# Twelve feed-forward tiles of the first two token blocks computed jointly by seven quarter products, and the softmax mixer's two heads interleaved

## The chip, the cores and the metric

The kernel runs on one core of a Trainium2 chip. The metric is the device time of one execution in microseconds (us); lower is better. Engines are named as in the profile: PE (TensorE matmul), PEld (its weight load), DVE (VectorE), ACT (ScalarE), POOL (GpSimd) and SP (SyncE, which issues DMAs).

## The reference

One layer of a hybrid decoder, for 2048 tokens of 1024 features in float32, with 16 meta tokens ahead of them:

```python
def hybrid_layer(h, pos, norm_mix_w, w_in, w_gate_up, b_gate, gla_norm_w, sinks,
                 w_out, norm_ff_w, w_ff1, w_ff2):
    u = rmsnorm(h, norm_mix_w)
    proj = u @ w_in
    gq, gk, gv, gr, glr, sq, sk, sv = jnp.split(proj, split_points, axis=-1)
    o_gla = gla_mixer(gq, gk, gv, gr, glr, w_gate_up, b_gate, gla_norm_w)   # gated linear attention, chunks of 64
    o_swa = swa_mixer(sq, sk, sv, sinks, pos)       # softmax in a window of 128, 8 heads in 2 groups
    h = h + jnp.concatenate([o_gla, o_swa], axis=-1) @ w_out
    f = rmsnorm(h, norm_ff_w)
    return h + jnp.square(jax.nn.relu(f @ w_ff1)) @ w_ff2                    # 1024 -> 4096 -> 1024
```

The result is the final rmsnorm of that, without the meta tokens.

## The kernel before

**Precision.** Every operand of a large product is split into a high and a low part, and a product of one 128-row k tile is three matmuls of 512 columns: high x high, high x low, low x high (`mm3`, lines 158 to 160). The split of a weight is one ACT pass (`wh`, line 123) and one DVE pass (`wl`, line 124).

**Blocks.** The tokens are four blocks of 512. The feed-forward layer has 32 tiles of 128 hidden units. For a block, a tile is `up` (8 k tiles, 24 matmuls into `psd`; then DVE `fr`, ACT square and high part, DVE low part `hid`, lines 1376 to 1384), and `down` takes groups of 8 tiles: for each of 8 output tiles 24 matmuls and a DVE add into `h` (line 1405).

**Stages, in the order of time.** Blocks 0 and 1 are projected with seven products of quarters (to 186 us). Then two mixer streams start, `gla` and `swa`, Python generators whose every `yield` is a place where the driver puts the next large product between; they run until 1147 us. Beside them go the projection of blocks 2 and 3 (`u`), the trunk of block 0 (output projection, up, down; 485 to 1006 us) and the first part of block 1's trunk (1006 to 1373 us). Then comes the tail: the output projection of blocks 2 and 3 (1373 to 1461), the last group of block 1's `down` as a cover for the preparation (to 1506), and blocks 2 and 3 jointly by quarters: `up` (1506 to 1811), `down` (class `Second`, 1811 to 2078) and a last piece.

**Quarters.** A product of a 2 x 2 arrangement (two blocks of tokens or two halves) by 2 x 2 quarters of the weight is done as seven products of sums of quarters in place of eight (up into `psq`, down into `psw`). DVE and ACT make the sums: for `up` those of the weight (`r`) and of the activations (`ops`), for `down` the operands `b` (hidden units' sums, which are stored to DRAM as `hops` by `to_ops` and loaded again by `load_b`) and the weight's (`rw`, line 2108). `close_0` to `close_2` finish a pair of tiles, `evict` (line 2165) adds a product into two or more results. The order within these stages is written out by hand: `W2.job(step, ...)` puts a load or a sum into a step, and `chain` gives the order of the first sums with a time for each.

**Softmax mixer.** For each of 16 blocks of 128 tokens and for each of two kv heads: `swa_scores` (four pairs of score matmuls `sc`, exponentials, on POOL four scalings `p`, line 997), then `swa_values` (transposes `tr` and `trm`, split into `ph` and `pl`, POOL's `affine_select` for the triangle, line 1026, three kinds of value matmuls into `pv`). The GLA mixer's POOL work is the copies `qpad` (line 1215) and eight scalings `AT` (line 1231). The score, transposed and norm tiles (`sc`, `tr`, `psn`) share two PSUM buffers.

**Queues.** Each engine runs its instructions in the order in which they were written; all DMAs are issued by SP in order.

Of the kernel before, what the change touches and what calls it, by code (L numbers as in the profile page):

```python
# [17 lines left out]
P = 128  # L18
# [12 lines left out]

F_SK, F_SQ, F_Q, F_K, F_R = 0, 1, 5, 7, 9
NFEAT = 13


class Layer:
# [80 lines left out]
    def split_w(self, src, n=1024):  # L117
        nc, wp = self.nc, self.wp
        raw = wp.tile([P, 1024], F32, name="raw", tag="raw")[:, :n]
        nc.sync.dma_start(out=raw, in_=src)  # L120
        wh = wp.tile([P, 1024], F32R, name="wh", tag="wh")[:, :n]
        wl = wp.tile([P, 1024], F32R, name="wl", tag="wl")[:, :n]
        nc.scalar.activation(wh, raw, AF.Copy)  # L123
        nc.vector.tensor_tensor(wl, raw, wh.bitcast(F32), ALU.subtract)  # L124
        return wh, wl
# [49 lines left out]
    def meta_prep(self, cp):  # L175
# [8 lines left out]
        for kt in range(KT):  # L184
            t = cp.tile([P, 48], F32R, name=f"um{kt}", tag=f"um{kt}")
# [6 lines left out]
        for kt in range(KT // 2):  # L192
            t = cp.tile([P, 48], F32R, name=f"umd{kt}", tag=f"umd{kt}")
# [731 lines left out]
    def swa(self, sp):  # L925
# [10 lines left out]
        yield  # L936
        yield
        yield
        for b in range(nblk):
# [60 lines left out]
    def swa_values(self, kv, sp, p, pm, lhs, oT):  # L1000
        nc = self.nc
        pt = self.px.tile([P, NB], F32, name="trm", tag="sx")

# [3 lines left out]
        for g in range(4):  # L1007
            d, s = self.ptm[:, g * P : (g + 1) * P], self.pm4.bitcast(F32)
            nc.scalar.activation(d, s, AF.Copy, scale=self.hmask[:, g : g + 1])
        pt = self.px.tile([P, NB], F32, name="tr", tag="sx")  # L1010
        c0 = 0 if len(lhs) == 2 else P + NM
        for g in range(4):
            nc.tensor.transpose(pt[:, g * P : (g + 1) * P], p[:, g, c0 : c0 + P], self.ident)
        ph = sp.tile([P, NB], F32R, name="ph", tag="ph")
        pl = sp.tile([P, NB], F32R, name="pl", tag="pl")
        nc.scalar.activation(ph, pt, AF.Copy)
        nc.vector.tensor_tensor(pl, pt, ph.bitcast(F32), ALU.subtract)
        yield
        yield
        pv = self.pm.tile([P, NB], F32, name="pv", tag="pv", bufs=1)  # L1020
        for i, v in enumerate(lhs):
            if i:

                for t in (ph, pl):
                    tv = t.rearrange("p (a b) -> p a b", a=4)
                    nc.gpsimd.affine_select(
                        tv, tv, pattern=[[0, 4], [1, P]], compare_op=ALU.is_ge, fill=0.0, base=0, channel_multiplier=-1
                    )
                yield
                yield  # L1030
                yield
            for t in (ph, pl):
                nc.tensor.matmul(pv, lhsT=v[:, kv, :], rhs=t, start=i == 0 and t is ph, stop=False)  # L1033
        nc.tensor.matmul(pv, lhsT=self.vm[:, kv, :], rhs=self.ptm, start=False, stop=True)
        ol = sp.tile([64, NB], F32, name="ol", tag="pl")
        nc.scalar.activation(ol, pv[64:P, :], AF.Copy)
        nc.vector.tensor_tensor(
            oT[64 * kv : 64 * kv + 64].rearrange("p a b -> p (a b)"), pv[0:64, :], ol, ALU.add
        )
        yield  # L1040
# [166 lines left out]
    def gla_pair(self, c, gp, qk, v):  # L1207
# [24 lines left out]
        yield  # L1232
        yield
# [97 lines left out]
    def out_proj(self, blk, mx, halloc, acc, after=None):  # L1331
# [3 lines left out]
        for m in range(KT):  # L1335
            w = self.split_w(a["wo"][m].rearrange("p k c -> p (k c)"))
# [3 lines left out]
            if self.finish and m == 0:  # L1340
                next(self.finish)
# [11 lines left out]
    def trunk(self, blk, ahead_of, hid_pair, last):  # L1353
# [6 lines left out]
        accs = [self.acc_tile()]  # L1360
        units = []
        hs = yield from self.out_proj(blk, mx[0], self.halves("h", F32, units), accs[0])
# [5 lines left out]
        hid = [[None] * 8 for _ in range(4)]  # L1368

        def up(ff):  # L1370
            w = self.split_w(a["w1"][ff].rearrange("p k c -> p (k c)"))
            ps = yield from self.product(w, lambda k: f[k])
            if not rb:
                rb.append(self.rstd_bc(accs[0]))
# [3 lines left out]
            if self.finish:  # L1378
                next(self.finish)
                if ff == 3:  # L1380
                    self.finish = None
            h, l = hid_pair(ff)
            nc.scalar.activation(h, r, AF.Copy)
            nc.vector.tensor_tensor(l, r, h.bitcast(F32), ALU.subtract)  # L1384
            hid[ff // 8][ff % 8] = (h, l)
            yield

        def final(acc):

            rf = self.rstd_bc(acc)  # L1390
            yield
            for m in range(KT):
                h = hs[m]
                nc.vector.scalar_tensor_tensor(h, h, self.nfin[:, m : m + 1], rf, ALU.mult, ALU.mult)
                nc.sync.dma_start(out=self.out[blk, :, m, :], in_=h)
                if m % 2:
                    yield

        def down(g):
            if g == 3:  # L1400
                accs[0] = self.acc_tile()
            for m in range(KT):
                w = self.split_w(a["w2"][g, m].rearrange("p k c -> p (k c)"))
                ps = yield from self.product(w, lambda k: hid[g][k])
                nc.vector.tensor_tensor(hs[m], hs[m], ps, ALU.add)
                if g == 3:
                    self.sumsq_add(hs[m], accs[0], m, fast=True)
                if g == (2 if last else 3) and m >= 4:
                    self.ahead = self.ahead or ahead_of()
                    for _ in range(3):  # L1410
                        next(self.ahead[0], None)
                yield

        yield from up(0)
        for g in range(4):
            for t in range(1, 8):
                yield from up(8 * g + t)
            if g < 3:
                yield from up(8 * g + 8)
            if last and g == 3:  # L1420
                continue
            self.half_way = last and g == 2
            yield from down(g)

        if last:
            self.left = hs, units, hid[3]
        else:
            self.finish = final(accs[0])


    def tail_pair(self, blks, ax, hb, pq):
# [3 lines left out]
        hs1, units1, hid3 = self.left  # L1435
        ahead, mx = self.ahead
        for _ in ahead:
            pass
        self.ahead = None
        lo_half, up_half = slice(0, NB), slice(NB, 1024)  # L1440
        two = lambda t: t.rearrange("p (k c) -> p k c", k=2)
        accs = [self.acc_tile() for _ in blks]
        hu, rb = [[], []], []
        ops = {n: [] for n in range(1, 8)}
        spots = {1: [ax] * 4, 2: [ax] * 4, 6: [ax] * 4, 5: [hb] * 4, 7: [ax] * 4, 4: [hb] + [None] * 3, 3: [None] * 4}

        def op_hi(n, src):
            h, l = self.unit("oh", F32R, spots[n].pop(0)), self.unit("ol", F32R, spots[n].pop(0))
            nc.scalar.activation(h, src, AF.Copy)
            for c in (lo_half, up_half):  # L1450
                ops[n].append((h[:, c], l[:, c]))
            return lambda: nc.vector.tensor_tensor(l, src, h.bitcast(F32), ALU.subtract)

        def normed(t, j):
            nc.vector.tensor_tensor(two(t), two(t), rb[j].unsqueeze(1).to_broadcast([P, 2, NB]), ALU.mult)
# [4 lines left out]
        def after(j):  # L1460
            done = []

            def then(m, h):
# [4 lines left out]
                if m == KT - 1:  # L1468
                    scale(m, h)
                if j == 1:  # L1470
# [11 lines left out]
                    elif m == 4:  # L1482
                        op_hi(2, hu[0][2])()
                        op_hi(2, hu[0][3])()

            return then

        for j in range(2):
            yield from self.out_proj(blks[j], mx[j], self.halves("h", F32, hu[j]), accs[j], after(j))


        cov_raw, cov_w = {}, {}

        def cov_load(t):
            cov_raw[t] = self.wp.tile([P, 1024], F32, name="raw", tag="raw")
            nc.sync.dma_start(out=cov_raw[t], in_=a["w2"][3, t].rearrange("p k c -> p (k c)"))

        def w_hi(src):
            wh = self.wp.tile([P, 1024], F32R, name="wh", tag="wh")
            wl = self.wp.tile([P, 1024], F32R, name="wl", tag="wl")  # L1500
            nc.scalar.activation(wh, src, AF.Copy)  # L1501
            return (wh, wl), lambda: nc.vector.tensor_tensor(wl, src, wh.bitcast(F32), ALU.subtract)

        def cov_split(t):
            cov_w[t], lo = w_hi(cov_raw[t])
            lo()

        cov_load(0)
        cov_load(1)
        cov_split(0)  # L1510
        with self.tc.manual_schedule():
            self.tail_ordered(
                blks, ax, hb, pq, hu, rb, accs, ops, op_hi, normed, w_hi, cov_load, cov_split, cov_w, two,
            )

    def tail_ordered(
        self, blks, ax, hb, pq, hu, rb, accs, ops, op_hi, normed, w_hi, cov_load, cov_split, cov_w, two
    ):
        nc, a = self.nc, self.a
        hs1, units1, hid3 = self.left  # L1520
# [9 lines left out]
        def w_load(j, i):  # L1530
            t = W.setdefault(j, {})[f"r{i}"] = raw_tile("r")
            nc.sync.dma_start(out=t, in_=a["w1"][2 * j + i].rearrange("p k c -> p (k c)"))
# [43 lines left out]
        def sum_1(u):  # L1576
            t1[u] = self.unit("t1", F32, ax)
# [9 lines left out]
        def sum_4(u):  # L1587
# [4 lines left out]
        chain = [  # L1592
            (3.0, 0, lambda: rb.append(self.rsqrt_of(psn))),
            (1.23, 0, lambda: normed(b12[0], 1)),
            (1.23, 0, lambda: normed(b12[1], 1)),
            (1.23, 0, lambda: normed(b22[0], 1)),
            (1.23, 0, lambda: normed(b22[1], 1)),
# [673 lines left out]
```

## Time and profile before

| | |
|---|---|
| median of 3 runs | 2134.22 us (2134.05 to 2135.95) |
| the profiled execution | 2136.22 us, of which the span of its instructions is 2134.5 us |
| mean granted TensorE clock | 0.996 |
| PE busy | 2116.9 us, 10283 instructions |
| DVE, ACT, POOL busy | 1497.7, 1035.7, 160.0 us |
| HBM read and written | 227.64 and 69.86 MB, 139 GB/s |

A busy engine is one with an instruction under way. Matmuls overlap one another, so that the mean duration of one is not the time it adds; the distance between starts is. The granted clock is the share of full speed that TensorE was given in a stretch.

### The profile page before, as it was taken

What the parts mean: (1) busy time and instruction counts of PE and PEld (TensorE: products, weight loads), DVE (VectorE), ACT (ScalarE), POOL (GpSimd) and SP (SyncE); (2) the same over time, 40 slices, a digit from 0 to 9 for tenths busy, and PEclk for the clock granted to TensorE, in tenths of its full rate; (3) what the DMA queues carried; (4) which work ended last, traced back from release to release, by engine and by line L of the source; (5) the groups of instructions that cost most, each with busy time, mean ns of one, the idle gap of its engine ahead of it and who ended that gap; (6) DMA issues with size and microseconds to landing.
All of it is one profiled execution on the core that took longest, in us unless ns stands there. A gap on an engine that the chain in (4) does not pass through costs nothing.

```text
span 2134.5 us, 28244 instructions
## 1 busy us (share of the span) xinstructions
PE 2116.9 (99%) x10283; PEld 1785.6 (84%) x10283; DVE 1497.7 (70%) x2535; ACT 1035.7 (49%) x1969; POOL 160.0 (7%) x284
## 2 busy tenths in 40 slices
PE   9999999999999999999999999999999999999998
PEld 7987799888888888888888888888888888888887
DVE  7867856777977778788864445466867776785876
ACT  6524545446664646466652323453544545333434
POOL 0000212111111212121110000000000000000000
PEclk9999999999999999999999999999999999999999
DMA  6436333435333333334423334644345557754422
GB/s 241 142 117 230 114 98 114 131 127 166 96 115 103 112 95 112 98 118 153 138 84 104 99 97 152 201 135 136 125 162 182 173 176 262 293 175 141 146 70 79
DMA packets 148795, 299.42 MB, mean 140 GB/s; under 512 B 14384, under 2 KB 62256, under 8 KB 148656
## 3 DMA queue, kind: packets, MB, share of 16 engines
q1 hardware_dynamic: 148656, 297.62, 42.9%
q8 instruction: 81, 1.33, 0.2%
q14 instruction: 58, 0.48, 0.1%
HBM read 227.64 MB, written 69.86 MB: 139 GB/s over the span
## 4 chain that ended last, share of the span: by engine, by line
PE 94%; DVE 3%; DMA 1%; ACT 1%; issue 0%; SPq 0%; POOL 0%; DVEq 0%; ACTq 0%
PE psd L158 17%; PE psd L160 17%; PE psd L159 17%; PE psq L160 6%; PE psq L158 6%; PE psq L159 6%; PE psw L158 4%; PE psw L159 4%; PE psw L160 4%; PE psv L625 2%; PE lv L1191 2%; PE pv L1033 1%; PE psd L431 1%; PE psd L432 1%; PE psd L433 1%; PE sc L972 1%
## 5 line engine op out<-in xcount | busy, mean ns | idle before, releaser
L123 ACT ACTIVATE wh<-raw 128x1024 fp32r<-128x1024 f32 (+1 forms) x175 | 184.3, 1053 | 348.0 <-PE psd L160 320.2
L124 DVE TENSOR_TENSOR wl<-raw,wh 128x1024 fp32r<-128x1024 f32 (+1 forms) x175 | 215.9, 1234 | 47.5 <-ACT wh L123 47.2
L158 PE MATMUL psd<-f,wh 128*128 128x512 f32 x512 | 203.3, 397 | 0.0
L158 PE MATMUL psd<-hid,wh 128*128 128x512 f32 x512 | 202.4, 395 | 0.0
L160 PE MATMUL psd<-hid,wh 128*128 128x512 f32 x512 | 199.9, 390 | 0.4 <-DVE hid L1384 0.4
L160 PE MATMUL psd<-f,wh 128*128 128x512 f32 x512 | 199.9, 390 | 0.0
L159 PE MATMUL psd<-f,wl 128*128 128x512 f32 x512 | 199.7, 390 | 0.0
L159 PE MATMUL psd<-hid,wl 128*128 128x512 f32 x512 | 199.5, 390 | 0.0
L158 PE MATMUL psw<-bh,wh 128*128 128x512 f32 x392 | 152.5, 389 | 0.0
L159 PE MATMUL psw<-bh,wl 128*128 128x512 f32 x392 | 152.5, 389 | 0.0
L160 PE MATMUL psw<-bl,wh 128*128 128x512 f32 x392 | 152.5, 389 | 0.0
L158 PE MATMUL psq<-oh,wh 128*128 128x512 f32 x384 | 149.8, 390 | 0.0
L160 PE MATMUL psq<-ol,wh 128*128 128x512 f32 x384 | 149.4, 389 | 0.0
L159 PE MATMUL psq<-oh,wl 128*128 128x512 f32 x384 | 149.4, 389 | 0.0
L158 PE MATMUL psd<-u,wh 128*128 128x512 f32 x320 | 131.0, 411 | 0.7 <-ACT wh L310 0.7
L159 PE MATMUL psd<-u,wl 128*128 128x512 f32 x320 | 127.3, 398 | 0.0
L160 PE MATMUL psd<-u,wh 128*128 128x512 f32 x320 | 127.1, 397 | 0.0
L1501 ACT ACTIVATE wh<-rw 128x1024 fp32r<-128x1024 f32 x49 | 52.0, 1061 | 149.7 <-PE psw L160 132.9
L160 PEld LDWEIGHTS psd<-hid,wh 128*128 128x128 f32 x512 | 96.1, 188 | 21.6 <-DVE hid L1384 0.8
L160 PEld LDWEIGHTS psd<-f,wh 128*128 128x128 f32 x512 | 96.1, 188 | 20.9
L158 PEld LDWEIGHTS psd<-f,wh 128*128 128x128 f32 x512 | 96.2, 188 | 19.3 <-issue 0.5
L159 PEld LDWEIGHTS psd<-f,wl 128*128 128x128 f32 x512 | 96.2, 188 | 19.2 <-issue 0.5
(422 smaller groups left out, 5071.1 us busy)
## 6 DMA issues: line engine op xcount, KB each, us to landing
raw<-w SPq DMA_DIRECT2D x132, 512.0 KB
b<-hops SPq DMA_DIRECT2D x49, 512.0 KB
raw<-wo SPq DMA_DIRECT2D x32, 512.0 KB
r<-w SPq DMA_DIRECT2D x32, 512.0 KB
rw<-w2q SPq DMA_DIRECT2D x28, 512.0 KB
hops<-t SPq DMA_DIRECT2D x42, 256.0 KB
feat<-st SPq DMA_DIRECT2D x36, 256.0 KB
raw<-wf SPq DMA_DIRECT2D x17, 512.0 KB
```

Of the source, the lines that this page charges most:

```text
L123: nc.scalar.activation(wh, raw, AF.Copy)
L124: nc.vector.tensor_tensor(wl, raw, wh.bitcast(F32), ALU.subtract)
L158: nc.tensor.matmul(ps, lhsT=wh, rhs=ah, start=first, stop=False, skip_group_check=skip)
L159: nc.tensor.matmul(ps, lhsT=wl, rhs=ah, start=False, stop=False, skip_group_check=skip)
L160: nc.tensor.matmul(ps, lhsT=wh, rhs=al, start=False, stop=last, skip_group_check=skip)
L431: nc.tensor.matmul(ps, lhsT=ah, rhs=wh, start=kt == 0, stop=False)
L432: nc.tensor.matmul(ps, lhsT=ah, rhs=wl, start=False, stop=False)
L433: nc.tensor.matmul(ps, lhsT=al, rhs=wh, start=False, stop=kt == KT - 1)
L625: nc.tensor.matmul(ps, lhsT=x, rhs=y[:, w], start=new and i == 0 and k == 0 and n == 0, stop=i == 1 and k == 1 and n == 2, skip_group_chec ...
L972: nc.tensor.matmul(ps, lhsT=qh, rhs=self.kr[:, 2 * kv, win], start=True, stop=False)
L1191: nc.tensor.matmul(ps[:, at : at + P], lhsT=k[:, hp, j * P : (j + 1) * P], rhs=ql[:, :, :, 1, :], start=True, stop=True)
L1501: nc.scalar.activation(wh, src, AF.Copy)
```

## The change

Blocks 0 and 1 now do only 20 of the 32 tiles on their own (`PLAIN`). Block 0's groups are 8, 8 and 4 tiles; block 1's are 8, 4 and 8. The hidden units of block 1's first group are stored to DRAM (`held`) and used at the tail as the cover that its last group was before; its last group is now the cover of a new joint stage. That stage does tiles 20 to 31 of both blocks by quarters with the routine of the tail (`ordered`, `Second` with one group of three pairs). Its inputs, the residuals after the output projection, are stored by the trunk (`hmid`, and `hpart` after its own down products), and are loaded, scaled, normed and split in `prefetch`, which takes a step in each of block 1's ups 15 to 19. The sums of hidden units go through `hops_j`. In its last steps the joint stage loads the mixers' results for the tail and splits the tail's first weight. Block 0's final scaling (`outputs`) now stands beside the tail's output projection.

In the softmax mixer, the transposes of the second head are written ahead of the first head's second value product; a block has 13 places where it had 17; `ph` and `pl` have two buffers; the mixer begins two places later. The eight `AT` scalings of the other mixer are split by a place into four and four.

```diff
+JOINT = 12
+PLAIN = 32 - JOINT
+GROUPS = (
+    [list(range(g, min(g + 8, PLAIN))) for g in range(0, PLAIN, 8)],
+    [list(range(0, 8))] + ([list(range(8, PLAIN - 8))] if PLAIN > 16 else []) + [list(range(PLAIN - 8, PLAIN))],
+)
+HALF_WAY = PLAIN - 6
...
         nxt = self.swa_prep(0, sp, ld, None)
-        yield
-        yield
-        yield
+        for _ in range(5):
+            yield
...
-            for kv in range(2):
-                yield from self.swa_values(kv, sp, *pk[kv], lhs, oT)
-                if kv == 0 and b + 1 < nblk:
-                    nxt = self.swa_prep(b + 1, sp, ld, vr)
+            ts = [self.swa_transposes(sp, pk[0][0], b > 0)]
+            self.swa_meta_part(pk[0][1])
+            yield
+            yield
+            pv = self.swa_first(0, ts[0], lhs)
+            if b + 1 < nblk:
+                nxt = self.swa_prep(b + 1, sp, ld, vr)
+            ts.append(self.swa_transposes(sp, pk[1][0], b > 0))
+            yield
+            yield
+            self.swa_second(0, ts[0], lhs, pv, oT)
+            self.swa_meta_part(pk[1][1])
+            yield
+            pv = self.swa_first(1, ts[1], lhs)
+            yield
+            yield
+            self.swa_second(1, ts[1], lhs, pv, oT)
+            yield
...
         for h in range(8):
             nc.gpsimd.tensor_scalar(AT[:, h, :], self.ident, dg[:, h : h + 1], 1.0, ALU.mult, ALU.mult)
-        yield
-        yield
+            if h % 4 == 3:
+                yield
...
+            if last and ff in groups[0]:
+                nc.sync.dma_start(out=self.held[ff], in_=t.bitcast(F32))
+            else:
+                hid[ff] = h, l
+            if last:
+                self.half_way = ff >= HALF_WAY
+                if ff > HALF_WAY:
+                    next(self.prefetch, None)
...
+        groups = GROUPS[blk]
+        done = 0
+        for g, group in enumerate(groups):
+            until = group[-1] + 2 if g < len(groups) - 1 else group[-1] + 1
+            while done < until:
+                yield from up(done)
+                done += 1
+            if not last or 0 < g < len(groups) - 1:
+                yield from down(g)
...
+        def prefetch():
+            load(0)
+            scale(0, 0)
+            yield
+            load(1)
+            norm(0, 0)
+            scale(0, 2)
+            yield
+            op(1, 0)
+            scale(1, 0)
+            norm(0, 2)
+            yield
+            scale(1, 2)
+            norm(1, 0)
+            op(2, 2)
+            yield
+            norm(1, 2)
+            self.cov_load(st, 0)
+            self.cov_load(st, 1)
+            yield
...
+        nj, j0, full = (16, 0, 14) if tail else (JOINT // 2, PLAIN // 2, JOINT // 2)
+        hops = self.hops if tail else self.hops_j
...
+        else:
+            W2 = Second(self, ax, hb, pq, (tuple(range(nj // 2)),), 1, PLAIN // 2, hops, (self.hpart[0], self.hpart[1]))
+            W2.add_mix(st)
...
+        if not tail:
+            to_ops(old, ((1, "s"), (2, "c11")))
+            W2.job(0, lambda: (close_1(old), to_ops(old, ((4, "t5"), (6, "t3")))), front=True)
+            W2.job(1, lambda: (close_2(old), to_ops(old, ((5, "u2"), (3, "t4")))), front=True)
...
+            self.finish = self.outputs(blks[0], hs[0])
+            self.left = hs[1], W2.wo
```

The instructions on each engine, as they are written, show where this puts the work. A row has the line, the operation, the output and its inputs, and the shape. PE has 9310 rows before and 9166 after.

POOL, from the start of the mixers on. Before (`p` is the softmax mixer's weights, `qpad` and `AT` the other mixer's):

```order
L1154 TENSOR_TENSOR wgr_1842<-wg_1843,wgh_1844 64x256
L997 TENSOR_SCALAR p_2053<-p_2053,sst_2054 128x128 x4
L1215 COPY qpad_1838<-qe_2242 64x512
L1216 COPY qpad_1838<-qe_2242 64x512
L1231 TENSOR_SCALAR AT_2303<-tabs_306,dg_2301 128x128 x8
L997 TENSOR_SCALAR p_2260<-p_2260,sst_2261 128x128 x4
```

POOL at the same place after:

```order
L1189 TENSOR_TENSOR wgr_1850<-wg_1851,wgh_1852 64x256
L1250 COPY qpad_1846<-qe_2231 64x512
L1251 COPY qpad_1846<-qe_2231 64x512
L1266 TENSOR_SCALAR AT_2279<-tabs_313,dg_2277 128x128 x8
L1025 TENSOR_SCALAR p_2236<-p_2236,sst_2237 128x128 x4
L1025 TENSOR_SCALAR p_2298<-p_2298,sst_2299 128x128 x4
```

The first softmax block's four scalings `p` have moved from ahead of the `qpad` copies to behind them and behind `AT`.

PE, the first output tile of block 0's last group. Before, the end of its eight k tiles (the last one is `hid_8115`):

```order
L158 MATMUL psd_8183<-hid_7975,wh_8179 128x512
L159 MATMUL psd_8183<-hid_7975,wl_8180 128x512
L160 MATMUL psd_8183<-hid_7975,wh_8179 128x512
L158 MATMUL psd_8183<-hid_8059,wh_8179 128x512
L159 MATMUL psd_8183<-hid_8059,wl_8180 128x512
L160 MATMUL psd_8183<-hid_8059,wh_8179 128x512
L158 MATMUL psd_8183<-hid_8115,wh_8179 128x512
L159 MATMUL psd_8183<-hid_8115,wl_8180 128x512
L160 MATMUL psd_8183<-hid_8115,wh_8179 128x512
```

PE, the same output tile after (the last tile's units are `hid_8169`):

```order
L173 MATMUL psd_8205<-hid_7417,wh_8201 128x512
L174 MATMUL psd_8205<-hid_7417,wl_8202 128x512
L175 MATMUL psd_8205<-hid_7417,wh_8201 128x512
L173 MATMUL psd_8205<-hid_7968,wh_8201 128x512
L174 MATMUL psd_8205<-hid_7968,wl_8202 128x512
L175 MATMUL psd_8205<-hid_7968,wh_8201 128x512
L173 MATMUL psd_8205<-hid_8068,wh_8201 128x512
L174 MATMUL psd_8205<-hid_8068,wl_8202 128x512
L175 MATMUL psd_8205<-hid_8068,wh_8201 128x512
L173 MATMUL psd_8205<-hid_8169,wh_8201 128x512
L174 MATMUL psd_8205<-hid_8169,wl_8202 128x512
L175 MATMUL psd_8205<-hid_8169,wh_8201 128x512
```

The newest hidden units are read as the fourth k tile instead of the eighth.

SP, the start of the quarter products down. Before, in the tail:

```order
L1743 DMA hops_80<-su_15409 128x512
L1743 DMA hops_80<-t4_15572 128x512
L2075 DMA b_15656<-hops_80 128x1024
L2082 DMA acc_15658<-hres_79 128x2x512
L2082 DMA acc_15660<-hres_79 128x2x512
```

SP after, in the new joint stage (`hops_j`), where the last pair's sums are stored once the down products have begun:

```order
L1924 DMA hops_j_81<-su_11679 128x512
L1924 DMA hops_j_81<-cc_11723 128x512
L1924 DMA hops_j_81<-t53_11834 128x512 x2
L2307 DMA b_11839<-hops_j_81 128x1024
L2302 DMA rw_11841<-w2q 128x2x512
L2302 DMA rw_11843<-w2q 128x2x512
L1924 DMA hops_j_81<-su_11679 128x512
L1924 DMA hops_j_81<-t4_11878 128x512
L2307 DMA b_11882<-hops_j_81 128x1024
```

The last stores of the pair now alternate with the loads of the steps, where before the one piece that had no pair (`hlast`) stood behind.

More of the change, by code (lines that the diff above doesn't have):

```diff
@@ L1367, in trunk @@
         rb = []
-        hid = [[None] * 8 for _ in range(4)]
+        hid = {}
         def up(ff):
@@ L1399, in down @@
[L1399 to L1411, printed above, removed]
-                yield
@@ L1414, in trunk @@
[L1414 to L1431, printed above, removed]
-        nc, a = self.nc, self.a
[L1435 to L1443, printed above, removed]
+                w = self.split_w(lambda t: self.w2_load(t, group, m), len(group) * P)
@@ new lines, in down @@
+                ps = yield from self.product(w, lambda k: hid[group[k]], len(group))
+                nc.vector.tensor_tensor(hs[m], hs[m], ps, ALU.add)
+                if g == len(groups) - 1:
+                    if m % 2:
+                        nc.sync.dma_start(out=self.hpart[0, :, m - 1 : m + 1, :], in_=two(units[m // 2]))
+                    if m >= 4:
+                        self.ahead = self.ahead or ahead_of()
+                        for _ in range(3):
+                            next(self.ahead[0], None)
@@ new lines, in down, with outputs @@
+                yield
+        groups = GROUPS[blk]
[7 more added lines that the diff above has]
+                yield from down(g)
+        self.left = units, [hid.get(ff) for ff in groups[-1]]
+    def outputs(self, blk, tiles):
+        nc = self.nc
+        acc = self.acc_tile()
+        for m in range(KT):
+            self.sumsq_add(tiles[m], acc, m, fast=True)
+            if m % 2:
+                yield
+        rf = self.rstd_bc(acc)
+        yield
+        for m in range(KT):
+            h = tiles[m]
+            nc.vector.scalar_tensor_tensor(h, h, self.nfin[:, m : m + 1], rf, ALU.mult, ALU.mult)
+            nc.sync.dma_start(out=self.out[blk, :, m, :], in_=h)
+            if m % 2:
+                yield
@@ new lines, in joint_run, with cov_load @@
+    def joint_run(self, st):
+        nc = self.nc
+        for _ in self.prefetch:
+            pass
+        self.cov_split(st, 0)
+        st["units"], st["hid"] = self.left
+        st["hs"] = [st["units"][m // 2][:, (m % 2) * NB : (m % 2 + 1) * NB] for m in range(KT)]
+        with self.tc.manual_schedule():
+            self.ordered(st)
+    def cov_load(self, st, t):
+        raw = st.setdefault("cov_raw", {})[t] = self.wp.tile([P, 1024], F32, name="raw", tag="raw")
+        self.w2_load(raw, st["cov"], t)
@@ L1469, in then @@
                     scale(m, h)
+                if j == 0 and m < 6 or j == 1:
+                    next(self.finish, None)
+                if j == 0:
+                    next(ahead, None)
+                    next(ahead, None)
                 if j == 1:
@@ L1705, in tail_ordered @@
         later = []
-        for of in (f_square, f_scale):
+        for of in (f_square, f_scale) if tail else ():
             for u in range(4):
@@ L1753, in close_2 @@
             TT(o["t4"], o["s"], o["u2"], ALU.subtract)
-        W2 = self.second(blks, ax, hb, pq, w_hi, two)
-        for j in range(16):
+        if tail:
+            W2 = Second(self, ax, hb, pq, ((0, 1, 2, 3), (4, 5, 6)), 0, 0, hops, (self.hres[0], self.hres[1]))
+            W2.add_last()
+        else:
+            W2 = Second(self, ax, hb, pq, (tuple(range(nj // 2)),), 1, PLAIN // 2, hops, (self.hpart[0], self.hpart[1]))
+            W2.add_mix(st)
+        for j in range(nj):
             o = {"j": j, "b0": bank(0), "b1": bank(1)}
-            nxt = j < 15
-            mids = old is not None and old["j"] < 14
+            nxt = j < nj - 1
+            mids = old is not None and old["j"] < full
             for slot, (n, b) in enumerate(((1, "b0"), (6, "b1"), (2, "b0"), (5, "b2"), (7, "b1"), (4, "b3"), (3, "b2"))):
```

463 lines of the change are left out of this document (297 added, 166 removed).

## The prediction

> **What bounds the kernel now.** I read the page's totals, then the chain that ended last, then what PE waited for, then tables by stage.
>
> ```profile
> span 2134.5 us, 28244 instructions
> PE 2116.9 (99%) x10283; PEld 1785.6 (84%) x10283; DVE 1497.7 (70%) x2535; ACT 1035.7 (49%) x1969; POOL 160.0 (7%) x284
> PE 94%; DVE 3%; DMA 1%; ACT 1%; issue 0%; SPq 0%; POOL 0%; DVEq 0%; ACTq 0%
> ```
>
> PE is busy for 2116.9 of 2134.5 us, and 94% of the chain that ended last is PE. So time leaves this kernel if PE's work leaves it, and comes back only where PE begins to wait. The list of PE's waits tells how little it waits today:
>
> ```profile
> PE sc L972 <- DVE nt L81: 2.8, 1, 2.8
> PE z L1080 <- POOL wgr L1154: 1.7, 1, 1.7
> ...
> PE psn L97 <- DVE pm L1006: 1.0, 1, 1.0
> PE pv L1033 <- DVE pl L1017: 0.8, 1, 0.8
> ...
> PE psd L160 <- DVE hid L1384: 0.4, 1, 0.4
> ...
> 193.22 0.39 PE L1080 MATMUL z<-lrT,wgr 128*128 128x16 f32 x2 [1.73 <-POOL wgr L1154]
> ```
>
> The two long ones lie early: the second at 193.2 us, as its row in the timeline says, the first at 232.8 us (row below). Everything later waits about 1 us at a time. What remains is how tight each stage is. The columns of the next view are: the stretch, its length, then busy time (and instructions) of PE, PEld, DVE, ACT, POOL, the granted clock, DMA share and GB/s.
>
> ```profile
> 255.00:1150.00 895.00, 892.81 (x4662) 763.32 (x4662) 667.40 (x1401) 487.18 (x1171) 143.53 (x251) 1.00 0.38 116
> 540.00:580.00 40.00, 40.00 (x207) 33.85 (x206) 37.76 (x81) 24.13 (x53) 2.80 (x7) 1.00 0.31 92
> 1161.30:1335.40 174.10, 174.10 (x770) 144.16 (x769) 79.13 (x92) 58.90 (x76) 0.00 (x0) 1.00 0.37 115
> 1505.80:1811.30 305.50, 305.50 (x1347) 252.67 (x1346) 217.55 (x289) 155.77 (x224) 0.00 (x0) 1.00 0.54 182
> 1811.30:1963.60 152.30, 152.30 (x673) 126.16 (x672) 108.99 (x106) 58.08 (x59) 0.00 (x0) 1.00 0.60 214
> 1963.60:2077.90 114.30, 114.30 (x506) 94.65 (x506) 84.64 (x87) 45.79 (x46) 0.00 (x0) 1.00 0.34 109
> ```
>
> The first row is the stretch with the mixers, the second the densest piece of it, the third plain feed-forward of block 1, the fourth the quarter products up, the last two the quarter products down. PE is full in all of them; DVE is the next engine everywhere.
>
> **What goes.** A plain tile costs 24 matmuls up (8 k tiles, three each for the split) and 24 down, so 12 tiles of two blocks are 12 x 2 x 48 = 1152. By quarters, 6 pairs of tiles times 7 products times 4 k tiles times 3 are 504 up, and 7 products times 4 output tiles times 6 k tiles times 3 are 504 down: 1008. So 144 matmuls of 512 columns go, with no other PE work added.
>
> ```profile
> L159 PE MATMUL psd<-f,wl 128*128 128x512 f32 x512 | 199.7, 390 | 0.0
> ```
>
> Their price is not the mean of one, 390 ns in this row of the page, since matmuls overlap. It is the distance from start to start: 174.10 / 770 = 0.2261 us in the plain stage, 305.50 / 1347 = 0.2268 and 152.30 / 673 = 0.2263 in the quarter stages. The quarter form has the same price as the plain one, so the gain is 144 x 0.2263 = **32.6 us**, all of it on the path, as PE is.
>
> **What may come back: the start of the mixers.** The early wait is worth reading, because the change moves what stands in front of it.
>
> ```profile
> 223.92 0.69 DVE L1214 TENSOR_TENSOR qe<-qk,decays 128x512 f32<-128x512 f32 x1
> 223.90 2.22 POOL L997 TENSOR_SCALAR p<-p,sst 128x128 f32<-128x128 f32 x4 [30.73 <-DVE vr L920]
> 226.06 0.60 POOL L1215 COPY qpad<-qe 64x512 f32<-64x512 f32 x1
> 227.37 0.63 ACT L1046 ACTIVATE sg<-r 128x512 f32<-128x512 f32 x1 [3.16 <-POOL qpad L1216]
> 232.79 0.49 PE L972 MATMUL sc<-kr,qs 128*128 128x144 f32 x1 [2.76 <-DVE nt L81]
> 232.00:234.00 2.00, 1.21 (x4) 1.11 (x5) 1.96 (x4) 1.16 (x3) 0.00 (x0) 0.58 0.67 158
> 234.00:236.00 2.00, 2.00 (x7) 1.52 (x6) 2.00 (x7) 1.15 (x2) 0.00 (x0) 0.50 0.67 225
> 236.00:238.00 2.00, 2.00 (x6) 1.60 (x5) 0.90 (x3) 0.86 (x2) 0.00 (x0) 0.50 0.70 270
> 238.00:240.00 2.00, 2.00 (x14) 1.82 (x12) 1.78 (x6) 1.57 (x3) 0.00 (x0) 0.71 0.02 6
> ```
>
> POOL scales the softmax mixer's first weights for 2.22 us; behind them stand the qpad copies; ACT's gate (sg) waits for those; ACT's and DVE's rsqrt steps stand behind the gate; and PE's second score matmul waits for their buffer. Then the granted clock falls to half for some 7 us: (0.42 + 0.50 + 0.50 + 0.29) x 2 = 3.4 us more. So this wait costs 6.2 us. The change starts the softmax mixer two places later, so the four scalings stand behind the copies. The copies can then follow qe, which ends at 223.92 + 0.69 = 224.61, so 1.45 us earlier than 226.06. A wait of about 1.3 us is left, and the 1.0 us waits of the list left the clock at 1.00 (first windows row). That gives 1.5 + 3.4 = 4.9. Against it the first block's eight score tiles now stand nearly together, where DVE is already full (1.96 and 2.00 of 2.00). I take -4; ends -6.2 (the wait gone whole) and +2.8 (one more such wait).
>
> [...]
>
> **The mixers' stretch.** 512 of the plain matmuls that ran between mixer instructions stand elsewhere now, so the mixers have 512 x 0.2263 = 116 us less to hide under: 779 us. DVE's work under them falls less. A product of 24 takes one wl and, up, one fr and one hid, or, down, one add:
>
> ```profile
> L124 DVE TENSOR_TENSOR wl<-raw,wh 128x1024 fp32r<-128x1024 f32 (+1 forms) x175 | 215.9, 1234 | 47.5 <-ACT wh L123 47.2
> L1376 DVE SCALAR_TENSOR_TENSOR fr<-psd,rb 128x512 f32<-128x512 f32 x64 | 44.0, 688 | 81.7 <-PE psd L160 81.5
> L1384 DVE TENSOR_TENSOR hid<-fr,hid 128x512 fp32r<-128x512 f32 x64 | 45.8, 717 | 0.8 <-ACT hid L1383 0.4
> L1405 DVE TENSOR_TENSOR h<-h,psd 128x512 f32<-128x512 f32 x56 | 38.5, 687 | 69.6 <-PE psd L160 69.3
> L2108 DVE TENSOR_TENSOR rw<-rw 128x1024 f32<-128x1024 f32 x28 | 34.1, 1219 | 0.0
> L2136 DVE TENSOR_TENSOR bl<-b,bh 128x1024 fp32r<-128x1024 f32 x49 | 59.7, 1218 | 0.0
> L2165 DVE TENSOR_TENSOR acc<-acc,psw 128x512 f32<-128x512 f32 x56 | 37.2, 685 | 9.3 <-PE psw L160 9.3
> ```
>
> That is 2.64 or 1.92 us, 21.3 products, 49 us. DVE goes from 667.4 / 895 = 75% to 618 / 779 = 79%. Here 540 to 580 shows 94% without any PE idle, and the list has only some 2 us of waits to win after 255 us, so the lower end is -2; the upper, 12, is four waits like the early one at their bare 2.8 us, plus the clock on one. I take +4, nearer to the row that waits nothing. The softmax mixer also goes from 17 to 13 places a block, with its two heads interleaved; whether that starves PE is a rival below. POOL's work is the same (143.5 of 895 us), only in another order.
>
> **Block 0's last group** now holds four tiles, so the last tile's hidden units are used as the fourth k tile: 11 matmuls (2.5 us) and eight small ones after they are begun. Before, 23 matmuls stood there, and they were just enough:
>
> ```profile
> 945.68 0.39 PE L160 MATMUL psd<-f,wh 128*128 128x512 f32 x1
> 951.92 1.11 DVE L1384 TENSOR_TENSOR hid<-fr,hid 128x512 fp32r<-128x512 f32 x1
> 953.09 0.50 PE L160 MATMUL psd<-hid,wh 128*128 128x512 f32 x1 [0.40 <-DVE hid L1384]
> ```
>
> From the last up matmul to hid's low half DVE, with its backlog, took 7.4 us. With some 3.3 us of cover the wait is between 0 (there are 0.4 us to win; no backlog: fr, ACT and hid alone take some 2 us) and 4.1. I take +2. It occurs once.
>
> **The preparation of the joint stage** lies in five ups of block 1: 12 more DVE passes of 1.22 us (14.6) beside 5 x 2.64 = 13.2 make 27.8 us of DVE in 5 x 24 x 0.2263 = 27.2 us of PE. Weights are split ahead into spare buffers, so little shows: +1, ends 0 and 3.
>
> **The joint stage.** Up, it is the tail's routine at the tail's rate: DVE 217.55 of 305.50 us there, 71%, no wait: 0. Down, 21 steps take 114 us of PE. DVE: 21 x (1.218 + 1.22) = 51, 28 evictions x 0.685 = 19, 12 weight sums x 1.22 = 15, with the closing of the last pair and the first passes for the tail by estimate 15 more (a dozen of 1.22 us): 100, 88%, and some 94% in the first 12 steps. The tail's own is 84.64 of 114.30, 74%. I take +1, ends 0 and 6. The last pair's operands go through memory: stored some 9 us after the last up product, needed at the fifth step, 27 us after it. A 256 KB store and its waiter took 4.7 us at most:
>
> ```profile
> 1379.82 0.33 SPq L1464 DMA_DIRECT2D hres<-h  x1
> 1384.55 0.72 ACT L1458 ACTIVATE h<-h,vecs 128x512 f32<-128x512 f32 x1 [3.86 <-DMA hres<-h]
> ```
>
> So 9 + 4.7 + 9.4 (twice that for the 512 KB load) = 23 of 27 us: hidden by four steps of other pairs; without them up to 14 us would stand open.
>
> **Nothing else.** Block 0's output scaling moves under the tail's output projection (16 DVE passes of 0.7 us, where 1161 to 1335 shows DVE at 45%); the eight held tiles, stored and loaded again (512 KB each), lie on queues at a DMA share of 0.37 to 0.60. If that cover failed, a load of 9.4 us would stand open once.
>
> **The sum.** -32.6 - 4 + 4 + 2 + 1 + 1 = -28.6 us. The profiled execution took 2136.2 us (span 2134.5 and 1.7 around it), 2.0 more than the median of 2134.2; taken off that median the forecast is 2105.6, said as **2106 us**, with 2100 to 2112 as its own range.
>
> **The rivals.**
> *No new waits*: early wait gone, nothing comes back: 2134.2 - 32.6 - 6.2 = 2095.4. For it speaks the list of waits, against it DVE at 94% in places that get tighter.
> *Joint stage bound by DVE*: if each of the first 12 steps down loses one weight pass (1.22 us), 14.6 more: 2121. For it speaks 94% there; against it that DVE at 94% went by unnoticed at 540.
> *Priced by the mean*: were a matmul worth its 390 ns, 144 would be 56 us, 2082 with what comes back. The windows speak against it: 770 in 174.1 us.
> *Slower: the softmax mixer's shorter chain.* With 13 places a block, transposes stand closer behind POOL's scaling. If in each of 16 blocks one head's 2.22 us of scaling stood open on PE, 16 x 2.22 = 35.5 us: 2141.5. From 28 / 16 = 1.8 us a block on, the kernel is no faster. Against it: in this list the mixers' values (pv) waited once, 0.8 us.
> *The gain eaten just so* by several of these, 2130 to 2138.5.
>
> **Chances.** Forecast 0.63; no new waits 0.12; joint stage bound by DVE 0.14; priced by the mean 0.03; slower 0.05; eaten 0.03. 0.2% (4.3 us) is about what a measurement of this kernel can tell from no change: faster 0.92, same 0.03, slower 0.05. The range, 2096 to 2122, takes in the forecast, most of the first rival and the second.
>
> **What would show it.** In the trace after: 144 fewer PE rows at 0.226 us from start to start; the score's wait near 230 us shorter and the clock at 1.00 behind it; DVE near 79% in the mixers' stretch with a few waits of 1 to 3 us; one wait at block 0's last group; the joint stage near 2 x 114 us with no wait over 2 us. I am wrong if PE shows waits on POOL's p, on tr or pv in most softmax blocks, or if the granted clock lies under 1.00 in a stage after 255 us.

## The result, and the profile after

| | before | after |
|---|---|---|
| median, us (4 runs each) | 2135.09 (2134.05 to 2136.09) | 2122.52 (2121.58 to 2127.24) |
| ratio, 95% interval | | 0.9946 (0.9928 to 0.9963) |
| profiled execution, its span | 2136.22, 2134.5 | 2122.51, 2120.8 |

The kernel became faster by 12.6 us. The sign was forecast, the size was not: 2106 was said, with 2096 to 2122, and 2122.5 lies just outside. (One later run of the kernel before, 3027 us at a mean granted clock of 0.654, is left out of all ratios.)

First the page of the kernel after, then the head of the list of PE's waits (us in total, how often, the longest).

```profile
span 2120.8 us, 28281 instructions
PE 2091.6 (99%) x10139; PEld 1758.8 (83%) x10139; DVE 1585.8 (75%) x2653; ACT 1077.5 (51%) x2031; POOL 153.7 (7%) x284
PE 86%; DVE 6%; DMA 3%; ACT 3%; issue 1%; POOL 1%; SPq 0%; DVEq 0%; ACTq 0%; POOLq 0%
```

```profile
PE tr L1045 <- POOL p L1025: 3.1, 3, 2.5
PE psq L173 <- ACT su L1979: 2.9, 2, 2.4
PE psd L173 <- ACT wh L138: 2.7, 1, 2.7
PE sc L1000 <- DVE sst L1002: 2.5, 2, 1.3
PE sc L1000 <- DVE nt L93: 1.9, 1, 1.9
```

The 144 matmuls are gone (10283 to 10139). But PE's share of the last chain fell from 94 to 86%, and four waits of about 2 to 3 us stand where there were two. Where they lie shows in the stages, first two of before (mixers' stretch; the tail's output projection), then the kernel after (mixers' stretch; joint up; joint down; the tail's output projection; the tail's quarter products up).

```profile
185.80:1147.50 961.70, 954.23 (x4931) 812.16 (x4931) 722.81 (x1529) 529.76 (x1267) 157.03 (x272) 0.99 0.38 118
1373.50:1461.40 87.90, 87.90 (x388) 72.44 (x387) 49.80 (x57) 41.60 (x54) 0.00 (x0) 1.00 0.54 178
```

```profile
183.90:1041.40 857.50, 842.09 (x4414) 716.40 (x4413) 664.31 (x1476) 493.48 (x1229) 150.73 (x272) 0.99 0.41 129
1123.40:1242.80 119.40, 116.50 (x506) 95.55 (x505) 76.84 (x100) 60.42 (x84) 0.00 (x0) 0.99 0.46 154
1242.80:1357.50 114.70, 114.69 (x505) 94.47 (x504) 92.18 (x101) 48.52 (x55) 0.00 (x0) 1.00 0.70 248
1357.50:1447.60 90.10, 89.41 (x389) 72.74 (x389) 68.04 (x85) 47.69 (x66) 0.00 (x0) 1.00 0.72 242
1492.00:1797.60 305.60, 305.60 (x1348) 252.85 (x1348) 216.87 (x288) 155.79 (x224) 0.00 (x0) 1.00 0.53 181
```

The mixers' stretch lost 517 PE rows, 117 us at 0.2263, but became only 104.2 us shorter: 12.8 given back. The joint up takes 119.4 us for 504 matmuls worth 114.1: 5.3. The joint down takes 114.7: 0.6. The tail's output projection takes 2.2 more; the rest of the tail is the same within 0.2. The input stage was 1.9 shorter, which the runs below show to be scatter: for the same code it ends at 183.8 to 184.4 us in three profiles in which the clock is 1.00 from 50 to 70 us (after, e5_newswa, e7_joint16), and at 185.4 to 185.8 in three in which it is 0.89 to 0.93 there (before, e3_both, e4_oldswa). Together 12.8 + 5.3 + 0.6 + 2.2 - 1.9 = 19.0, and 32.6 - 19.0 = 13.6 is the 13.7 us by which the span fell.

### The profile page after: what moved, and what is told of

It is laid out like the page before. It is cut to its first block, busy times and chain, and to the rows that moved or that the text cites. A ratio compares the mean times of both kernels' runs of the same rounds, so it can differ in the third digit from the quotient of the medians.

```text
span 2120.8 us, 28281 instructions
## 1 busy us (share of the span) xinstructions
PE 2091.6 (99%) x10139; PEld 1758.8 (83%) x10139; DVE 1585.8 (75%) x2653; ACT 1077.5 (51%) x2031; POOL 153.7 (7%) x284
## 4 chain that ended last, share of the span: by engine, by line
PE 86%; DVE 6%; DMA 3%; ACT 3%; issue 1%; POOL 1%; SPq 0%; DVEq 0%; ACTq 0%; POOLq 0%
PE psd L173 11%; PE psd L175 11%; PE psd L174 11%; PE psq L173 7%; PE psq L174 7%; PE psq L175 7%; PE psw L175 6%; PE psw L173 6%; PE psw L174 6%; PE psv L640 2%; PE lv L1226 2%; PE psd L446 1%; PE psd L447 1%; DVE wl L139 1%; PE psd L448 1%
## 5 line engine op out<-in xcount | busy, mean ns | idle before, releaser
L138 ACT ACTIVATE wh<-raw 128x1024 fp32r<-128x1024 f32 (+3 forms) x126 | 125.2, 995 | 158.3 <-PE psd L175 136.8
L139 DVE TENSOR_TENSOR wl<-raw,wh 128x1024 fp32r<-128x1024 f32 (+3 forms) x126 | 147.5, 1171 | 33.0 <-ACT wh L138 32.4
L1479 DVE TENSOR_TENSOR wl<-rw,wh 128x1024 fp32r<-128x1024 f32 x70 | 85.6, 1223 | 70.8 <-ACT wh L1478 70.7
L173 PE MATMUL psd<-hid,wh 128*128 128x512 f32 x320 | 128.8, 402 | 0.1
L173 PE MATMUL psd<-f,wh 128*128 128x512 f32 x320 | 128.1, 400 | 0.0
L174 PE MATMUL psd<-hid,wl 128*128 128x512 f32 x320 | 126.1, 394 | 0.3 <-DVE wl L139 0.3
L175 PE MATMUL psd<-hid,wh 128*128 128x512 f32 x320 | 126.0, 394 | 0.0
L175 PE MATMUL psd<-f,wh 128*128 128x512 f32 x320 | 125.4, 392 | 0.0
L174 PE MATMUL psd<-f,wl 128*128 128x512 f32 x320 | 125.2, 391 | 0.0
L175 PEld LDWEIGHTS psw<-bl,wh 128*128 128x128 f32 x560 | 105.2, 188 | 22.5 <-DVE bl L2368 0.7
L174 PEld LDWEIGHTS psw<-bh,wl 128*128 128x128 f32 x560 | 105.2, 188 | 21.9
L173 PEld LDWEIGHTS psw<-bh,wh 128*128 128x128 f32 x560 | 105.1, 188 | 21.6
```

Of the source, the lines that this page charges most:

```text
L173: nc.tensor.matmul(ps, lhsT=wh, rhs=ah, start=first, stop=False, skip_group_check=skip)
L174: nc.tensor.matmul(ps, lhsT=wl, rhs=ah, start=False, stop=False, skip_group_check=skip)
L175: nc.tensor.matmul(ps, lhsT=wh, rhs=al, start=False, stop=last, skip_group_check=skip)
```

## The experiments

Ratios are to the kernel before, run on the same chip; "after" is the changed kernel.

**The price of a matmul (e6_price).** The kernel before, with its order:

```diff
+        if self.short:
+            nc.tensor.matmul(ps, lhsT=wl, rhs=ah, start=False, stop=last, skip_group_check=skip)
+            return
...
+            self.short = last and ff >= 22
             ps = yield from self.product(w, lambda k: f[k])
```

> The kernel before with 144 large matmuls left out and nothing else moved: the third of the three (low part by high part) of block 1's ups 22 to 31 and of its third down group, in the stretch where only plain feed-forward runs; that part of the product is missing from the result. Theory (start-to-start price): 144 x 0.2263 = 32.6 us less than before, 2102 us. Rival (the price is the mean duration, 390 ns): 56 us less, 2078.5. Rival (weights, splits and loads are then the bound): less than 25 us, with waits for wl or wh in that stretch.

Measured: 2102.72 us, ratio 0.9855 (0.9838 to 0.9871): 32.0 us less, 0.222 us for each of the 144. The gain was priced rightly; 390 ns is not the price, and what is missing was given back elsewhere.

**Block 0's group of four (e1_groups).**

```diff
-    [list(range(g, min(g + 8, PLAIN))) for g in range(0, PLAIN, 8)],
+    [list(range(0, 8)), list(range(8, PLAIN - 8)), list(range(PLAIN - 8, PLAIN))],
```

The reason lies in these rows of the kernel after, at the change from block 0 to block 1: SP's issue, ACT's split of that weight, PE's first matmul on it; then the table by stretches, with the clock behind it (0.50).

```profile
846.23 0.33 SPq L135 DMA_DIRECT2D raw<-wo  x1
852.46 1.06 ACT L138 ACTIVATE wh<-raw 128x1024 fp32r<-128x1024 f32 x1 [3.47 <-DMA raw<-wo]
853.57 0.80 PE L173 MATMUL psd<-m,wh 128*128 128x512 f32 x1 [2.73 <-ACT wh L138]
```

```profile
854.00:856.00 2.00, 2.00 (x6) 1.52 (x6) 1.45 (x3) 0.46 (x1) 0.56 (x1) 0.50 0.96 375
```

From the load's issue to ACT's split 6.2 us passed. In a group of eight, the three weight buffers reach three products of 5.4 us ahead; in a group of four a product is half as long, and the same buffers reach half as far.

> The changed kernel with block 0's groups in the order 8, 4, 8 tiles instead of 8, 8, 4; nothing else. Theory (the group of four next to a new stage): with four tiles a product of down lasts 12 matmuls, 2.7 us, and the three weight buffers then reach 8 us ahead instead of 16; the first output projection weight of block 1, issued at 846.2 us, landed at 852.4, and PE stood for 2.7 us and then ran 3.4 us' worth at half clock. With a group of eight last the wait goes: 6 us less, about 2116.5 us. Rival A (the wait belongs to the weight ring behind any group of four): it moves to the up behind the group of four, 0 to -1.5 us, 2121 to 2122.5. Rival B (DVE's backlog bounds the stretch): a wait removed comes back as others, within 1 us of 2122.5.

Measured: 2116.73 us, ratio 0.9920 (0.9905 to 0.9934): 5.8 less than after. ACT's split of that weight now waits for PE, no longer for the load, and PE comes to it 6.4 us later without a wait:

```profile
846.84 1.06 ACT L138 ACTIVATE wh<-raw 128x1024 fp32r<-128x1024 f32 x1 [0.82 <-PE psd L175]
853.26 0.40 PE L173 MATMUL psd<-m,wh 128*128 128x512 f32 x1
```

The wait did not move to the up behind the group of four (rival A), and DVE did not bring it back (rival B).

**The joint stage's first products (e2_gates).**

```diff
-                (0, 0, lambda: hi(4, 0, b21[0])),
+                (0, 0, lambda: hi(4, 0, b21[0]), 18),
...
-                (0, 0, lambda: hi(3, 0, b22[0])),
+                (0, 0, lambda: hi(3, 0, b22[0]), 19),
...
                 if j == 0:
+                    now = 16 + slot
                     need(n)
```

The list of first sums is paced by a budget. While a gate holds an entry back, the budget grows, and behind the first product it let six high parts (`oh`) go, two and then the four below, ahead of the copy `su` that product 2 needs. After:

```profile
1127.02 3.88 ACT L1509 ACTIVATE oh<-hu 128x1024 fp32r<-128x1024 f32 x4
1130.81 0.57 ACT L1979 ACTIVATE su<-psq 128x512 f32<-128x512 f32 x1
1131.43 0.56 PE L173 MATMUL psq<-oh,wh 128*128 128x512 f32 x1 [2.44 <-ACT su L1979]
```

> The changed kernel with two numbers in the joint stage's list of first sums: the high parts of operands 4 and 3 may be written only at the third and fourth product, not all behind the first. Nothing else. Theory: six high parts (ACT, 0.97 us each) were written in one go ahead of su, the copy that frees the first product's bank; PE waited 2.4 us for su and ran at half clock behind it, 1.7 us more. With the gates the first wait goes: 4 us less, about 2118.5 us; the joint stage's up takes 115.3 instead of 119.4 us. Rival (ACT and DVE have that work in any case before the first pair ends, so it is late elsewhere): a wait of 1 to 3 us at another product, 2121 to 2123 us.

Measured: 2116.01 us, ratio 0.9916 (0.9899 to 0.9933): 6.5 less than after, with single runs from 2112.5 to 2119.6. In the trace the stage takes 115.1 us, 4.3 less than after, and the two stand in the other order:

```profile
1121.17 0.58 ACT L1980 ACTIVATE su<-psq 128x512 f32<-128x512 f32 x1
1121.64 3.89 ACT L1509 ACTIVATE oh<-hu 128x1024 fp32r<-128x1024 f32 x4
```

```profile
1117.50:1232.60 115.10, 114.64 (x506) 94.47 (x506) 76.82 (x100) 60.46 (x84) 0.00 (x0) 1.00 0.48 161
```

The remaining 2 us lie within the scatter; the profiled run is the fastest of the four, and in it the weight's wait of the last experiment was 1.7 us, with the clock at 1.00 behind it.

**Both (e3_both, and again as e12_both2).**

> Both edits together: groups 8, 4, 8 in block 0 and the gates. Theory (each wait stands for itself and costs its length and the half clock behind it): the sum, 10 us less than the changed kernel, about 2112.5 us, 0.9895 of the kernel before. Rivals: with the wait moved on behind the group of four 2117 to 2118.5; with DVE's backlog as the bound 2120 to 2122.

> Both edits again, the same kernel as e3_both, on the chip of the three runs above, so that differences of 1 to 4 us are read on one chip. Expected 2113 us, 0.990 of the kernel before.

Measured: 2112.96 us, 0.9899 (0.9884 to 0.9913), and on another chip 2114.89, 0.9905 (0.9889 to 0.9921). The two waits cost 7.6 to 9.6 us of the 19; singly they were 5.8 and 6.5, 12.3 together. Within the scatter that adds up; the measurement of both at once is the safer price.

**The softmax mixer's shorter chain (e4_oldswa, e5_newswa).** The first is after with the mixer of before, the second the kernel before with the mixer of after.

> The changed kernel with the softmax mixer as it was before (heads one after the other, 17 places a block, start two places earlier); the joint stage and all else stay. Theory (the shorter chain is what lets the mixers end within the shorter stretch): 16 blocks x 4 places = 64 more places, of which the stretch has none left, since the mixers already end at the last product of their stretch (1041 us); the last blocks then run with no large product beside them. At 0.5 to 1.5 us a place that is 30 to 90 us more, 2150 to 2210 us. Rival (the mixers have slack, and the interleaved heads are what costs the 13 us that the stretch gave back): 5 to 13 us less than the changed kernel, 2109 to 2117 us.

> The kernel before with the softmax mixer of the change alone (heads interleaved, 13 places a block, start two places later; the meta tokens' tiles lie in the change's pool, which makes the room). No joint stage, the same 8660 large matmuls. Theory (crowding: fewer large matmuls beside the same mixer work bring the small waits, here because the mixers run in a shorter stretch and end near 1000 instead of 1147 us): 5 to 8 us more than before, 2140 to 2143. Rival A (the interleaved heads are neutral, the waits come from the plain tiles' removal alone): within 1.5 us of 2134.6. Rival B (the interleaved chain waits less by itself): 3 us less or better.

Measured: 2133.78 us, 0.9995 (0.9985 to 1.0005), and 2138.03 us, 1.0019 (1.0009 to 1.0028). In the joint kernel the old chain costs 11.3 us more; both theories missed the size. The mixers then end at 1074 instead of 1041 us, and a weight of the cover comes late:

```profile
PE psd L173 <- ACT wh L1458: 9.0, 1, 9.0
```

```profile
1100.00:1110.00 10.00, 5.18 (x11) 3.75 (x12) 8.18 (x8) 4.02 (x5) 0.00 (x0) 0.50 0.45 157
```

9.0 us of wait (to 1104.4) and, from there to 1110, half of 5.6 us by the clock: 12, as much as the whole difference. The match is in part luck, for there is more on both sides: between 1000 and 1110 us PE stood idle for 13.3 us in all, while the weight's wait at 852 us does not occur in this kernel.

The late weight is the cover's fourth; 72 matmuls on the first three had run. ACT splits it at 1103.26 us, directly behind passes of the joint stage's preparation (`prefetch`). The preparation's loads are issued at 1078.3 us there and at 1045.4 in after, each time some 4 us behind the mixers' end. In after the ups of block 1 still follow and cover it; with the old chain PE has done them by then, and it falls on the cover. In the code its buffers (`ax`) lie where the mixers' pools have just been closed; that these hold the loads back was not tested alone.

By itself the new chain costs 3.3 us, less than the 5 that crowding was to cost and more than the 1.5 of no effect. So it saves no time of its own; it lets the mixers end in time for the preparation. My 30 us or more was too much: I had priced the 64 places as naked and nothing else, but with the old chain less mixer work stands between the same large matmuls earlier on (block 1's output projection begins at 838 instead of 854 us).

**Sixteen joint tiles (e7_joint16).** `JOINT = 16` with the gates.

> The version with the gates and 16 joint tiles instead of 12 (groups 8 and 8 in both blocks, so no group of four): 192 matmuls fewer than before, 48 fewer than with 12 tiles. Theory (the mixers' stretch is already full with 12): it loses another 384 large matmuls, 87 us or 32 places of 12 matmuls, to cover the mixers, and the mixers' last 32 places run with nothing beside them; with 12 joint tiles and the old mixer's 64 more places it took 30 us from 1041 to where the next up began. So some 15 us more for the naked places and 10.9 less for the matmuls: 2113 + 4 = 2117 us. Rival (only PE's matmuls count): 2113 - 10.9 = 2102 us. Rival (naked places and cold clock, 1.5 us each): 2140 us or more.

Measured: 2125.71 us, 0.9961 (0.9946 to 0.9975), 12.7 more than with twelve and both edits, though 48 matmuls fewer. The cause has the form of the last one, larger:

```profile
PE psd L173 <- ACT wh L1478: 11.6, 1, 11.6
```

It is the cover's fourth weight again, behind the preparation, whose loads are issued at 999.9 us, when the ups are over (PE begins the cover at 995.4). Behind the wait the clock stood at 0.50 until 1030 us, 3.1 us more. That is 14.7 of the 23.6 us to explain (12.7, and 10.9 for the 48 matmuls); the rest is spread over smaller waits. My 2117 came too low: it counted places without cover, not a preparation that comes late with half a clock behind it.

**The mixers' start (e8_start3, e9_first, e11_start7).** On top of both edits:

```diff
-        for _ in range(5):                 # e8, e9: 3; e11: 7
             yield
...
+            if b == 0:                     # e9 alone, ahead of the transposes
+                yield
+                yield
             ts = [self.swa_transposes(sp, pk[0][0], b > 0)]
```

> The version with both edits (8, 4, 8 and the gates), and the softmax mixer started after 3 places again instead of 5; all else of the interleaving stays. It tests the term of the start: with 5 places POOL's first scalings moved behind the qpad copies, but tr then waited 2.5 us for them at 240 us. Theory (the wait only changed its place): within 1.5 us of 2113, with sc waiting about 2.8 us near 230 us and no wait of tr near 240. Rival A (the late start costs): 3 to 5 us less. Rival B (it gains, as the prediction had it): 3 to 5 us more.

> Both edits (8, 4, 8 and the gates), the softmax mixer started after 3 places, but two more places inside its first block ahead of the transposes, so that blocks 1 to 15 stand where they stand with a start after 5 places. Theory (the 4 us of the start after 3 places came from how the two mixers' places meet in all later blocks, not from the start): as with 5 places, 2112 to 2114 us, and 2 to 4 us less if the wait of tr for POOL's scaling near 240 us (2.6 us) goes with the two places, 2109 to 2111. Rival (the cost lies in the first block): 2117 us, with the start's waits longer.

> Both edits, and the softmax mixer started after 7 places instead of 5. Theory (how the places of the two mixers meet decides the small waits; 3 places took 4 us more than 5): a change of 2 to 6 us in either direction without any change in the work; the mixers may end two places later, at 1 to 2 us. Rival (the late start itself gains): 2 to 4 us less than 2113.

Measured: e8 2117.04 us, 0.9919 (0.9905 to 0.9934); e9 2107.31, 0.9872 (0.9856 to 0.9887); e11 2112.65, 0.9894 (0.9879 to 0.9910). After and e9, PE's waits between 222 and 246 us:

```profile
229.03 0.33 PE L1000 MATMUL sc<-kr,qs 128*128 128x144 f32 x1 [1.87 <-DVE nt L93]
242.60 1.37 PE L1045 MATMUL tr<-tabs,p 128*128 128x128 f32 x4 [2.55 <-POOL p L1025]
235.91 6.28 POOL L1266 TENSOR_SCALAR AT<-tabs,dg 128x128 f32<-128x128 f32 x8 [12.34 <-DVE sst L1006]
```

```profile
230.13 0.49 PE L1003 MATMUL sc<-kr,qs 128*128 128x144 f32 x1 [2.77 <-DVE nt L93]
```

After, the first block's scalings stand behind all eight `AT` scalings (6.3 us), and PE's transposes wait for them. With the scores early and the transposes where they were, that wait is gone and the score's is back. e9 beside e12_both2, on one chip, is 7.6 us less, more than expected. The two profiles differ by 5.3 us, and only 1.9 of it is less idle time of PE in the 95 us behind the input stage (5.8 instead of 7.7); where the rest comes from is not shown. In e8 the start was no worse than in e3_both (8.2 and 8.3 us idle in those 95), but waits of 1.7 and 2.6 us came later, at 444 and 967 us. Its 4.1 us miss the theory and are rival B's in size, but not for its reason: the later waits point to how the two mixers' places meet in the later blocks, and e9, where these stand as in e3_both, has neither. e11 moved the start by two places more and measured nothing clear.

**Block 0's final rsqrt one place later (e10_outputs),** on top of e9:

> As the run before, and block 0's final rsqrt one place later beside the tail's output projection, so that its sums of squares are done before PE comes to them. Theory: the wait of psn for acc (0.3 to 1.8 us at 1376 us) goes: 0.5 to 1.5 us less than without it. Rival (nothing measurable): within 0.5 us.

Measured: 2109.86 us, 0.9875 (0.9857 to 0.9892), single runs from 2105.0 to 2112.8. In the time nothing shows; the scatter is larger than the effect looked for. In the trace the wait of `psn` for `acc` is gone, and PE has no idle time from 1360 to 1440 us.

The best version is e9: 2107.3 us, 27.3 less than before and some 15 less than the change as it was.

## Why the prediction was off

The terms that come back were to be 4 us and are 19.0 in the profiles: 15 us too few. The start makes up 6 of them, block 0's last group 3.8, the mixers' stretch 1, the joint up 5.3 and the tail's output projection 2.2; the preparation, the joint down and the input stage take 3.3 off again. The sign of being wrong that the prediction named did appear: the granted clock was 0.50 at 854 us and again from 1132 to 1134 us, behind the wait at 1129 us, both after 255 us.

- **The gain, -32.6:** right; 32.0 when measured alone.
- **The start, -4:** this term failed; nothing was gained, and in after some 2 us were lost. In the 95 us behind the input stage PE stood idle for 5.4 us before and for 6.9 to 8.3 in the five profiles with this order (after, e1_groups, e2_gates, e3_both, e12_both2). With half of the time at half clock added it is 10.2 before, 12.0 in after and 9.5 to 13.4 in the other four. The copies did follow `qe`, as read (at 222.31 us, directly behind its end). But the rest of the chain to the score's buffer stayed: the score's wait is 1.9 us in after and from 0.7 to 3.6 in the other four, and in after the clock was at half for 3.4 us behind it, where 1.3 us without a half clock were said. And I let the scalings move behind the copies and did not ask what waits for the scalings: `tr`, behind eight `AT`. Its 2.55 us is the end that I gave as +2.8 and did not take.
- **Block 0's last group, +2:** the wrong wait. I priced the hidden units' wait, which does not appear after; the weight's load, which halves its lead there, cost 5.8 us.
- **The mixers' stretch, +4:** of the 12.8 us 5.8 are that weight and 2 the start. Some 5 remain, near what was said. Of these 3.4 are short waits, of at most 1.3 us: PE's idle time between 280 and 840 us rose from 0.8 to 4.2 us. DVE is at 77.5% (664.31 / 857.5; 79% was said); that its load is the cause of these waits was not tested.
- **The joint up, 0:** failed, at +5.3. I took over the tail's rate because it is the same routine; its list of first sums is another one, and the order on ACT, not DVE's load (64% there, 71% was said), made the wait. By the profile of after it and the weight's load cost 11.1 us; taken out together they gave 7.6 to 9.6.
- **The preparation, +1, and the joint down, +1:** 0 and 0.6. DVE was busy for 80% of the joint down (92.18 / 114.70), not the 88% that were said, and that was hidden; the operands' way through memory too. The preparation is hidden only because the mixers end before the ups do: e4_oldswa and e7_joint16 show what it costs otherwise. The rival of a stage bound by DVE was wrong; that its time, 2121, came out nearly right is chance.
- **Nothing else:** the tail's output projection took 2.2 more. PE waits there for block 0's sums of squares (0.3 to 1.9 us in these runs). e10 took that wait away in the trace, but what it is worth in time was not resolved.

What a wait cost beside its own length differed: behind the weight's wait of 2.73 us in after the clock was at half for 6.8 us, 3.4 us more; behind `tr`'s 2.55 us for 3.4, 1.7 us more; behind the same 2.55 us in e2_gates for none. Still open: some 5 us between e9 (2107.3) and the kernel before less 32.0 (2102.6); the tail's 2.2 and the chain's 3.3 would fill it, but were not taken out one by one in that version.

## What to carry to other kernels

Where PE is full, price removed matmuls by their distance (here 0.226 us, where the mean of one is 390 ns; 0.222 when measured alone), and then look for new waits at the joints between stages, not in averages: the three that were looked into were each a matter of order (a weight buffer's lead in time, a burst ahead of a copy, a scaling behind another's). When a group gets smaller, the lead of every ring that counts products gets shorter with it. When an instruction moves back in a queue, ask who waits for it, not only who stood behind it. And when work is prepared under another stage, ask what has to end before it can begin: here the mixers' end decided whether the preparation was free.

## What the runs showed of the hardware

The same wait costs differently from run to run. In after and in e2_gates, `tr` waited 2.55 us, until 242.6 and 242.2 us; these are the microseconds 245 to 250 of the two, in that order:

```profile
245.00:250.00 5.00, 5.00 (x18) 3.71 (x17) 3.10 (x9) 3.44 (x15) 1.41 (x4) 0.73 0.00 0
```

```profile
245.00:250.00 5.00, 5.00 (x24) 3.82 (x23) 4.65 (x10) 4.52 (x14) 2.22 (x4) 1.00 0.00 0
```

In after the clock fell to half for a while (0.73 over these 5 us), in e2_gates it did not (1.00). Over the runs' profiles a wait of 1.2 to 4.2 us was followed by no half clock, or by some 3.4 or 6.8 us of it: in after one of 1.25 us at 201 us by 3.4, in e9 one of 1.6 us at 190 us by 3.4, in before one of 2.76 us at 233 us by 6.8, in e4_oldswa one of 2.6 us between 230 and 240 us by none. The half clock may begin within the wait: in after it is 0.50 from 852 us on, and the weight's wait ends at 853.57. And it came without a wait of PE too: in before the clock is 0.83 from 55 to 65 us, where PE is busy throughout. So the length of a wait alone did not decide it; what did was not shown. This may be a part of why four runs of one kernel lie up to 8 us apart (e10_outputs) and thirteen runs of before 5.1 and 5.5 us; that was not tested.
